# Pinning a root chain, summing modulation columns in pairs, and moving the odd blocks' sums in a two-layer trunk on one core

## The chip, the cores and the metric

The kernel runs on one core of a Trainium2 chip. A core has TensorE (matrix products), VectorE, ScalarE and GpSimd (element-wise work), SyncE, which issues the DMA transfers here, an on-chip memory (SBUF) and a small accumulation memory for TensorE's results (PSUM). The engines run side by side and wait for each other through semaphores. Each takes its own instructions strictly in the order in which they were written, so an instruction that waits holds everything behind it on its engine.

The metric is the device time of one execution in microseconds (us). Lower is better.

## The reference

The input x has 1024 tokens of 1024 numbers, the conditioning c has 1024. Two layers follow. Each has a mixer (layer A: an mLSTM, layer B: latent attention) and a feed-forward part (MLP) with a squared ReLU, each between two root-mean-square norms and each shifted, scaled and gated by vectors that are computed from c. Cut to what the change touches:

```python
c_act = jax.nn.silu(c)
for layer in range(DEPTH):
    sh1, sc1, g1, sh2, sc2, g2 = jnp.split(c_act @ mod_w[layer] + mod_b[layer], 6, axis=-1)
    h = modulate(rms_norm(x, norm_g[layer, 0]), sh1, sc1)
    y = mlstm_mixer(h, ...) if layer < N_A else mla_mixer(h, ...)
    x = x + g1[:, None, :] * rms_norm(y, norm_g[layer, 1])
    h = modulate(rms_norm(x, norm_g[layer, 2]), sh2, sc2)
    y = sq_relu_mlp(h, ffn_w1[layer], ffn_w2[layer])
    x = x + g2[:, None, :] * rms_norm(y, norm_g[layer, 3])
```

Here `modulate(h, shift, scale)` is `h * (1 + scale) + shift`, and `rms_norm` multiplies a token by one over the root of its mean square, then by a gain. All of it is computed in float32.

## The kernel before, in words

**Numbers and tiles.** Tokens are handled in 8 blocks of 128, features in 8 columns of 128 (`KD`). A float32 product is made of three products of a shorter type: each operand is split into a high half (a rounded copy, made by ScalarE) and a low half (the rest, made by VectorE), and `mm3` (L152) adds high times high, high times low and low times high. In the trace these are the lines L155, L156 and L157. Operands in SBUF live in 52 equal units (`U`). PSUM holds two wide tiles (`MM`, 1024 numbers, two banks) and four narrow ones (`SM`, 512 numbers, one bank).

**Order.** The program is traced from top to bottom, and a planner then writes the order of each engine: it runs a simulated clock with estimated costs and gives an engine that is free, by that clock, the earliest traced instruction that is ready. The order is fixed when the kernel is built. Two instructions of one engine can therefore stand in another order than in the source, and what the planner's clock held for ready can be late on the chip. `issue_after(ins)` is a request to the planner: instructions traced inside it are kept behind `ins` if they are of the same engine as `ins`.

**The front (`layer_a`, from L897).** The first four blocks of x are loaded (L407), then the weights that give shift and scale of the first norm, as four slabs of 2 MB: a slab has two neighbouring columns of shift and of scale, in eight transfers (`slab`, L961). ScalarE squares and sums each block (L926); VectorE turns the four sums of squares into inverse roots by a chain of small steps (`rsqrt`, L159 to L173); ScalarE scales the blocks with them (L930). Columns 0 and 1 of shift and scale are computed on TensorE, by 64 small matrix instructions with one column of c each (L995). Columns 2 to 7 are computed by `mod_sum` on VectorE: eight steps for a column, one for each 128 rows of the weights, each on 256 numbers (shift and scale), in two alternating accumulators (L982, L984), added by GpSimd (L985); TensorE then sums over the partitions (L992). `mod_col` (L988) adds the bias and the gain (L997, L999). `turned(k)` (L1001) does `mod_col`, transposes column k of the four blocks on TensorE (L183), applies scale and shift on ScalarE (L937) and splits the result into halves (L105, L106). The loop over k then feeds the value projection of the four blocks, 12 products a column, in four `SM` tiles that stay occupied until the last column (L1044). At k = 4 to 7 the other four blocks of x are loaded. At k = 7 a set of small constants (`late_consts`: positions, gate biases, norms) is loaded. After the loop come the evacuations of the values (`values`, `put_v`, L920) and the norm of the other four blocks.

**The mixers' last products.** After the mixer's core, each block n of a given order (0, 2, 4, 6, 1, 3, 5, 7) gets an output product (`out_proj`, 48 matrix instructions into an `MM` tile). In layer A its operand is first gated, transposed and split (`gate_split`, L1330, with L1338); three such blocks are traced ahead of the first product. `mixer_out` (L1145) follows each product: residual and norm (L178, L401, L402), store, and from time to time the norm of two finished blocks for the MLP (`h_norm`, L489: squares L494, root chain, scaling L497), after blocks n = 1, 3 and 5.

**The MLP.** It is a fast matrix scheme with seven products for a two-by-two cut of the operands. The token blocks are cut into even ones (0, 2, 4, 6) and odd ones (1, 3, 5, 7). `h_turn` (L444) transposes two blocks and applies shift and scale (L457). Even blocks are used as they are (left operands A11, A12), odd blocks also in sums with the even ones: `odd_sums` (L469, with L476 to L479) makes S1, S2, S3 and S4 on VectorE by four steps; `odd_high` and `odd_low` split them (L438, L442). Blocks 1 and 3 are the first odd pair (`odd_...(0)`), blocks 5 and 7 the second (`odd_...(2)`). While the odd blocks are made ready, TensorE runs the products that need even blocks alone: two products for each p from 0 to 7 (`up`, `up_product`, 24 matrix instructions for a p), whose results are taken out by L697 (ScalarE) and L690 (VectorE). Products 2 and 5 use two narrow tiles, the others one wide tile. In `mlp_begin` (L633) the odd blocks' steps are traced between these products. `w_first` (L504, L507, L509) and `w_step` (L540 to L589) load and split the weights, with some sums on GpSimd (L562, L563, L575, L582). Layer A and layer B share all of this code; in layer B the outputs' operands are split without a gate.

Of the kernel before, what the change touches and what calls it, by code (L numbers as in the profile page):

```python
# [21 lines left out]
P = 128  # L22
# [43 lines left out]
class Trunk:  # L66
# [31 lines left out]

    def SM(self):
        return self.pp.tile([P, 512], F32, tag="sm", name=self.nm("sm"), bufs=4)  # L100


    def split(self, hi, lo, src):
# [529 lines left out]
    def mlp_begin(self, l, odd):  # L633

        self.us = [self.dp.tile([P, 8 * 512], F32, name=f"us{l}_{p}", tag=f"us{l}_{p}") for p in range(self.NP)]
        self.ups = {}
        def up(p, *firsts):
            self.up_product(p, 1)
            self.up_product(p, 2)
            for f in firsts:  # L640
                next(self.first[f], None)

        self.odd_sums(0)
        up(0, 3, 4, 5)
        self.h_norm(5, 7)
        self.odd_high(0, "S2", "S3")
        up(1, 4, 5, 6)
        self.odd_high(0, "S1", "A22", "S4")
        self.odd_low(0, "S2", "S3")
        up(2, 5, 6, 7)  # L650
        self.odd_turn(2, [odd.pop(5), odd.pop(7)])
        self.odd_low(0, "S1", "A22", "S4")
        up(3, 6, 7)
        self.odd_sums(2)
        up(4, 7)
        self.odd_high(2, "S2", "S3", "S1")
        self.w_step()
        up(5)
        self.odd_high(2, "A22", "S4")
        self.odd_low(2, "S2", "S3")  # L660
        self.w_step()
        up(6)
        self.w_step()
        self.odd_low(2, "S1")
        self.w_step()
        up(7)
        self.w_step()
        self.odd_low(2, "A22", "S4")
        self.w_step()

    def up_product(self, p, s):
# [2 lines left out]
        S, V, G = self.S, self.V, self.G  # L674
        lo, hi = slice(0, 512), slice(512, 1024)
        if p not in self.ups:
            self.ups[p] = {"ps": None if p in (2, 5) else self.MM(), "x": [self.U("x")[:, :1024], None]}
        st = self.ups[p]
        ps = st["ps"][:, (lo, hi)[s - 1]] if s in (1, 2) and st["ps"] is not None else self.SM()
        w = self.w_take((0, p), s)  # L680
# [216 lines left out]
    def layer_a(self):  # L897
# [25 lines left out]
        def normed(xs, on_act=False):  # L923
            ssq = self.W("ssqs", [P, 4])
            for i, x in enumerate(xs):
                S.activation(self.U("h")[:, :D], x, AF.Square, accum_out=ssq[:, i : i + 1])  # L926
            r = self.rsqrt(ssq[:, : len(xs)], len(xs), 1.0 / D)
            for i, x in enumerate(xs):
                if on_act:
                    S.activation(x, x, AF.Copy, scale=r[:, i : i + 1])  # L930
                else:
                    V.tensor_scalar(out=x, in0=x, scalar1=r[:, i : i + 1], scalar2=None, op0=ALU.mult)

        def modulate(k, src, t, hi, lo, on_act):

# [35 lines left out]

            return slabs[k // 2][i // 2][:, i % 2, :, (k % 2) * P : (k % 2 + 1) * P]

        def mod_sum(k):

            u = self.U("acc")
            accs = [u[:, o : o + 2 * P].rearrange("p (s c) -> p s c", s=2) for o in (0, 2 * P)]
            for i in range(KD):
                src, acc = slab_part(k, i), accs[i % 2]
                c = self.cact[:, i : i + 1]  # L980
                if i < 2:
                    V.tensor_scalar(out=acc, in0=src, scalar1=c, scalar2=None, op0=ALU.mult)  # L982
                else:
                    V.scalar_tensor_tensor(out=acc, in0=src, scalar=c, in1=acc, op0=ALU.mult, op1=ALU.add)  # L984
            G.tensor_tensor(out=accs[0], in0=accs[0], in1=accs[1], op=ALU.add)  # L985
            sums[k] = accs[0]

        def mod_col(k, acc, ps):  # L988

# [28 lines left out]
            slab(2 * g)  # L1018
            self._raw()
        slab(6)  # L1020
        normed(xs[:4], True)
        for k in range(2, 4):
            mod_sum(k)
        w, acc = [], [None] * 4
        turned(0)
        for k in range(KD):
            if 1 <= k < 4:
                self._raw()
# [1 line left out]
                load_xs(k, k + 1)  # L1030
            if k == KD - 1:
                late = self.late_consts()
                next(late)
            if k % 3 == 0:
                w.append(self.take(("v", 0, k // 3)))
            if k + 4 < KD:
                mod_sum(k + 4)
            if k + 1 < KD:
                turned(k + 1)
            for tb in range(4):  # L1040
                if k == 0:
                    acc[tb] = self.SM()
                o = (k % 3) * VP
                self.mm3(acc[tb][:, :VP], self.hT_tb(hT, tb, k), tuple(u[:, o : o + VP] for u in w[k // 3]), k == 0, k == KD - 1)  # L1044
# [78 lines left out]
        finish(mods)  # L1123
        del hT
        order = self.ORDER
        pre = deque(self.gate_split(t, hn[t], sg) for t in order[:2])
        self.mixer_start(0, x_in, "x1")
        self.ahead, self.early = 0, 0
        w_out = [self.take(("wout", k)) for k in range(KD)]
        for n in range(NT):  # L1130
            if n + 2 < NT:
                pre.append(self.gate_split(order[n + 2], hn[order[n + 2]], sg))
            self.mixer_out(n, self.out_proj(pre.popleft(), w_out))


    ORDER = (0, 2, 4, 6, 1, 3, 5, 7)
# [8 lines left out]
    def mixer_out(self, n, y):  # L1145
# [4 lines left out]
        if n in (3, 5):  # L1150
            j = n - 3
            self.h_even(j, [hs.pop(t) for t in (2 * j, 2 * j + 2)])
        elif n == NT - 1:
            self.odd_turn(0, [hs.pop(1), hs.pop(3)])
        if n + 1 < NT:
            nxt = self.ORDER[n + 1]
# [2 lines left out]
        self.dma(out=x_out[tb * P : (tb + 1) * P, :], in_=xn)  # L1159
        if n in (1, 3, 5):  # L1160
            self.h_norm(*self.ORDER[n - 1 : n + 1])
        for p in range(self.BEGUN):
            if 0 <= n - 3 - p < 3:
                next(self.first[p], None)
# [684 lines left out]
```

## Time and profile before

| | us |
|---|---|
| median of 3 runs | 2317.43 (2316.24 to 2317.79) |
| the profiled execution, its own time | 2319.99 |
| its span in the trace | 2318.2 |
| TensorE busy | 2217.4 (96%) |
| VectorE busy | 1745.9 (75%) |
| ScalarE busy | 1012.0 (44%) |
| GpSimd busy | 472.0 (20%) |

PE stands for TensorE, PEld for its loading of weights, DVE for VectorE, ACT for ScalarE, POOL for GpSimd, SP for SyncE. L155 is line 155 of the kernel; where a helper records the instruction, the line is the helper's, and the names of the tiles tell the place. A row of waits reads "who waited <- for whom: total us, times, longest". A row of the timeline begins with its start and its length in us; in brackets stands the idle time of the engine before it and what ended that. A row of a table of stretches has, after the length, busy time and number of instructions for PE, PEld, DVE, ACT and POOL, then the granted TensorE clock as a share of full speed, the busy share of the DMA engines, and GB/s. A row of a group ends with its total busy time, the mean of one in ns, and the idle time before it. Ends of matrix instructions overlap, so the distance of two starts is the pace. A run's time is 1.8 us longer than the span of its trace here.

### The profile page before, as it was taken

The page shows a single profiled execution, that of the slowest core. Times are in us where ns is not written, and L with a number is a line of the kernel's source. Part 1 is how long each engine was busy: PE and PEld are TensorE (multiplying, and loading weights), DVE is VectorE, ACT ScalarE, POOL GpSimd, SP SyncE. Part 2 cuts the span into 40 slices and gives each one's busy share as a digit, 9 for nine tenths or more (in the row PEclk, how much of TensorE's full clock was granted, in tenths as well). Part 3 has the DMA queues.
Part 4 walks back from the last instruction along what each step waited for, and adds up shares of the span by engine and source line. Part 5 has one row for each costly group of instructions (what it writes and reads, how often), then busy time and mean ns, then how long its engine had stood idle before and what let it go on. Part 6 is the DMA issues. An engine that isn't in the chain of part 4 may idle for free. (4 is left out here: it accounts for less than half of the span.)

```text
span 2318.2 us, 29189 instructions
## 1 busy us (share of the span) xinstructions
PE 2217.4 (96%) x10786; PEld 1851.1 (80%) x10786; DVE 1745.9 (75%) x2792; ACT 1012.0 (44%) x1641; POOL 472.0 (20%) x322
## 2 busy tenths in 40 slices
PE   6999999998999999999999999999999999999998
PEld 5888887887777877777798989988777888777776
DVE  4585687667987767888999676665679877588888
ACT  3431366464444454333244545554634444633321
POOL 1000020003443333331021000000035433333300
PEclk9999999999999999999999999999999999999999
DMA  8376543143774465445322000022347545544452
GB/s 274 118 265 209 167 130 119 46 142 99 247 255 143 150 196 163 130 141 156 113 89 59 12 13 15 29 81 93 117 132 236 191 143 192 168 132 146 139 174 100
DMA packets 300070, 320.19 MB, mean 138 GB/s; under 512 B 16040, under 2 KB 252184, under 8 KB 299928
## 3 DMA queue, kind: packets, MB, share of 16 engines
q1 hardware_dynamic: 299928, 318.33, 43.4%
q8 instruction: 85, 1.39, 0.2%
q14 instruction: 57, 0.47, 0.1%
HBM read 245.85 MB, written 72.43 MB: 137 GB/s over the span
## 5 line engine op out<-in xcount | busy, mean ns | idle before, releaser
L155 PE MATMUL mm<-whi,uh 128*128 128x512 f32 x688 | 272.8, 397 | 12.6 <-DVE y L770 10.8
L157 PE MATMUL mm<-whi,ul 128*128 128x512 f32 x688 | 271.0, 394 | 1.2 <-DVE ul L764 1.2
L156 PE MATMUL mm<-wlo,uh 128*128 128x512 f32 x688 | 271.4, 394 | 0.0
L582 POOL TENSOR_TENSOR tt<-raw,tt 128x512 f32<-128x512 f32 x60 | 112.4, 1873 | 632.6 <-DVE wlo L555 632.6
L770 DVE TENSOR_TENSOR y<-y,mm 128x1024 f32<-128x1024 f32 (+1 forms) x161 | 193.2, 1206 | 49.7 <-PE mm L157 49.4
L155 PE MATMUL sm<-hSh,whi 128*128 128x512 f32 x544 | 216.2, 397 | 8.2 <-DVE x L690 7.9
L156 PE MATMUL sm<-hSl,whi 128*128 128x512 f32 x544 | 214.9, 395 | 0.0
L157 PE MATMUL sm<-hSh,wlo 128*128 128x512 f32 x544 | 213.8, 395 | 0.3 <-DVE wlo L555 0.3
L764 DVE TENSOR_TENSOR ul<-u,uh 128x896 fp32r<-128x896 f32 (+1 forms) x120 | 151.0, 1289 | 32.0 <-ACT uh L758 24.4
L555 DVE TENSOR_TENSOR wlo<-raw,whi 128x1024 fp32r<-128x1024 f32 x104 | 157.0, 1510 | 17.9 <-ACT whi L551 17.8
L690 DVE TENSOR_TENSOR x<-x,sm 128x512 f32<-128x512 f32 x196 | 130.9, 681 | 51.0 <-PE sm L157 48.1
L155 PEld LDWEIGHTS mm<-whi,uh 128*128 128x128 f32 x688 | 129.2, 188 | 49.2 <-DVE y L770 17.3
L562 POOL TENSOR_TENSOR tt<-raw,raw 128x512 f32<-128x512 f32 x32 | 57.3, 1791 | 496.9 <-PE sm L157 290.4
L157 PEld LDWEIGHTS mm<-whi,ul 128*128 128x128 f32 x688 | 129.2, 188 | 32.2 <-DVE ul L764 2.1
L156 PEld LDWEIGHTS mm<-wlo,uh 128*128 128x128 f32 x688 | 129.2, 188 | 29.3
L758 ACT CAST uh<-u 128x896 fp32r<-128x896 f32 (+1 forms) x120 | 108.0, 946 | 84.9 <-PE mm L157 66.8
L693 ACT ACTIVATE x<-x 128x1024 f32<-128x1024 f32 x64 | 67.8, 1059 | 149.6 <-DVE x L690 149.4
L155 PEld LDWEIGHTS sm<-hSh,whi 128*128 128x128 f32 x544 | 102.5, 188 | 35.4 <-DVE x L690 6.6
L265 DVE SCALAR_TENSOR_TENSOR acc<-modw,cact,acc 128x1024 f32<-128x1024 f32 x84 | 117.3, 1397 | 9.4 <-DMA modw<-in_kv_mod_w_dram 5.8
L551 ACT CAST whi<-tt 128x1024 fp32r<-128x1024 f32 x60 | 62.9, 1048 | 139.1 <-issue 62.2
L157 PEld LDWEIGHTS sm<-hSh,wlo 128*128 128x128 f32 x544 | 102.6, 189 | 25.2 <-DVE wlo L555 1.0
L587 ACT CAST w<-tt 128x512 fp32r<-128x512 f32 x60 | 37.2, 619 | 193.4 <-POOL tt L582 189.9
(407 smaller groups left out, 5975.2 us busy)
## 6 DMA issues: line engine op xcount, KB each, us to landing
raw<-in_ffn_w_dram SPq DMA_DIRECT2D x144, 512.0 KB, 4.9
u<-us SPq DMA_DIRECT2D x112, 448.0 KB, 4.2
us<-x SPq DMA_DIRECT2D x92, 512.0 KB, 2.6
modw<-in_mod_w_dram SPq DMA_DIRECT2D x80, 512.0 KB, 5.4
x<-xn SPq DMA_DIRECT2D x24, 512.0 KB, 3.3
x<-x SPq DMA_DIRECT2D x24, 512.0 KB, 4.0
x<-in_x_dram SPq DMA_DIRECT2D x16, 512.0 KB, 6.6
slab<-in_mod_w_dram SPq DMA_DIRECT2D x32, 256.0 KB, 5.9
```

Source lines behind the costliest of these rows:

```text
L155: mm(out, a[0], b[0], start=start, stop=False)
L156: mm(out, a[0], b[1], start=False, stop=False)
L157: mm(out, a[1], b[0], start=False, stop=stop)
L265: self.V.scalar_tensor_tensor(out=acc, in0=t, scalar=self.cact[:, k : k + 1], in1=acc, op0=ALU.mult, op1=ALU.add)
L551: S.copy(x[0], u)
L555: V.tensor_tensor(out=x[1], in0=u, in1=x[0].bitcast(F32), op=ALU.subtract)
L582: G.tensor_tensor(out=t1, in0=b21, in1=t2, op=ALU.subtract)
L690: V.tensor_tensor(out=dst, in0=src, in1=ps, op=ALU.add)
L693: S.activation(u, u, AF.Relu)
L758: S.copy(x[0], u)
L764: V.tensor_tensor(out=x[1], in0=u, in1=x[0].bitcast(F32), op=ALU.subtract)
L770: V.tensor_tensor(out=dst, in0=dst, in1=ps, op=ALU.add)
```

## The change

Five edits, in three places.

- **Front, order.** `normed` returns the last instruction of its root chain, and the first modulation sums and turns are traced inside `issue_after` of it: what they put on VectorE stays behind the chain. The late constants' loads are kept behind the load of block 7.
- **Front, sums.** `mod_sum(k, n)` sums n neighbouring columns at once, with one accumulator and no addition on GpSimd. Column 1 is summed alone, and 2 and 3, 4 and 5, 6 and 7 as pairs, with steps of 512 numbers. Column 0 alone stays on TensorE. Columns are turned in pairs.
- **Mixer A's last products.** Only the first block is gated ahead of the first product; the second and third are gated behind it.
- **Both mixers' last two products.** The first odd pair is turned after the seventh product (n = 6) and not after the eighth, and its sums and the halves of S2 and S3 are traced there, between the last two products. Blocks 5 and 7 are normed singly, each after its own residual. In `mlp_begin` the remaining steps of the odd blocks move up accordingly.
- **Products.** Product 6 also uses two narrow tiles.

```diff
-        self.odd_sums(0)
         up(0, 3, 4, 5)
-        self.h_norm(5, 7)
-        self.odd_high(0, "S2", "S3")
+        self.odd_high(0, "S1", "A22", "S4")
         up(1, 4, 5, 6)
-        self.odd_high(0, "S1", "A22", "S4")
-        self.odd_low(0, "S2", "S3")
-        up(2, 5, 6, 7)
         self.odd_turn(2, [odd.pop(5), odd.pop(7)])
         self.odd_low(0, "S1", "A22", "S4")
+        up(2, 5, 6, 7)
+        self.odd_sums(2)
         up(3, 6, 7)
-        self.odd_sums(2)
+        self.odd_high(2, "S2", "S3", "S1")
         up(4, 7)
-        self.odd_high(2, "S2", "S3", "S1")
+        self.odd_low(2, "S2", "S3")
+        self.odd_high(2, "A22", "S4")
...
-            self.ups[p] = {"ps": None if p in (2, 5) else self.MM(), "x": [self.U("x")[:, :1024], None]}
+            self.ups[p] = {"ps": None if p in (2, 5, 6) else self.MM(), "x": [self.U("x")[:, :1024], None]}
...
             r = self.rsqrt(ssq[:, : len(xs)], len(xs), 1.0 / D)
+            ins = self.last()
...
+            return ins
...
-        def mod_sum(k):
+        def mod_sum(k, n):
-            u = self.U("acc")
-            accs = [u[:, o : o + 2 * P].rearrange("p (s c) -> p s c", s=2) for o in (0, 2 * P)]
+            acc = self.U("acc")[:, : 2 * n * P].rearrange("p (s c) -> p s c", s=2)
+            o = (k % 2) * P
             for i in range(KD):
-                src, acc = slab_part(k, i), accs[i % 2]
+                src = slabs[k // 2][i // 2][:, i % 2, :, o : o + n * P]
...
-            G.tensor_tensor(out=accs[0], in0=accs[0], in1=accs[1], op=ALU.add)
-            sums[k] = accs[0]
+            for j in range(n):
+                sums[k + j] = acc[:, :, j * P : (j + 1) * P]
...
-        normed(xs[:4], True)
-        for k in range(2, 4):
-            mod_sum(k)
+        with self.tc.issue_after(normed(xs[:4], True)):
+            mod_sum(1, 1)
+            turned(0)
+            turned(1)
+            mod_sum(2, 2)
         w, acc = [], [None] * 4
-        turned(0)
...
                 late = self.late_consts()
-                next(late)
+                with self.tc.issue_after(self.last()):
+                    next(late)
...
-            if k + 4 < KD:
-                mod_sum(k + 4)
-            if k + 1 < KD:
+            if k % 2 and k + 1 < KD:
                 turned(k + 1)
+                turned(k + 2)
+                if k + 3 < KD:
+                    mod_sum(k + 3, 2)
...
-        pre = deque(self.gate_split(t, hn[t], sg) for t in order[:2])
+        pre = deque([self.gate_split(order[0], hn[order[0]], sg)])
...
-            if n + 2 < NT:
+            if 0 < n < NT - 2:
                 pre.append(self.gate_split(order[n + 2], hn[order[n + 2]], sg))
-            self.mixer_out(n, self.out_proj(pre.popleft(), w_out))
+            y = self.out_proj(pre.popleft(), w_out)
+            if n == 0:
+                pre.extend(self.gate_split(t, hn[t], sg) for t in order[1:3])
+            self.mixer_out(n, y)
...
-        elif n == NT - 1:
+        elif n == 6:
             self.odd_turn(0, [hs.pop(1), hs.pop(3)])
...
         if n in (1, 3, 5):
             self.h_norm(*self.ORDER[n - 1 : n + 1])
+        elif n >= 6:
+            self.h_norm(tb)
+        if n == 6:
+            self.odd_sums(0)
+            self.odd_high(0, "S2", "S3")
+            self.odd_low(0, "S2", "S3")
```

More of the change, by code (lines that the diff above doesn't have):

```diff
@@ L100, in SM, with last @@
         return self.pp.tile([P, 512], F32, tag="sm", name=self.nm("sm"), bufs=4)
+    def last(self):
+        return self.nc.cur_bb.bb.instructions[-1]
     def split(self, hi, lo, src):
@@ L641, in up @@
                 next(self.first[f], None)
-        self.odd_sums(0)
         up(0, 3, 4, 5)
-        self.h_norm(5, 7)
-        self.odd_high(0, "S2", "S3")
+        self.odd_high(0, "S1", "A22", "S4")
         up(1, 4, 5, 6)
-        self.odd_high(0, "S1", "A22", "S4")
-        self.odd_low(0, "S2", "S3")
-        up(2, 5, 6, 7)
         self.odd_turn(2, [odd.pop(5), odd.pop(7)])
         self.odd_low(0, "S1", "A22", "S4")
+        up(2, 5, 6, 7)
+        self.odd_sums(2)
         up(3, 6, 7)
-        self.odd_sums(2)
+        self.odd_high(2, "S2", "S3", "S1")
         up(4, 7)
-        self.odd_high(2, "S2", "S3", "S1")
+        self.odd_low(2, "S2", "S3")
+        self.odd_high(2, "A22", "S4")
         self.w_step()
         up(5)
-        self.odd_high(2, "A22", "S4")
-        self.odd_low(2, "S2", "S3")
+        self.odd_low(2, "S1")
         self.w_step()
@@ L663, in mlp_begin @@
         self.w_step()
-        self.odd_low(2, "S1")
+        self.odd_low(2, "A22", "S4")
         self.w_step()
@@ L667, in mlp_begin @@
         self.w_step()
-        self.odd_low(2, "A22", "S4")
         self.w_step()
@@ L972, in slab_part @@
             return slabs[k // 2][i // 2][:, i % 2, :, (k % 2) * P : (k % 2 + 1) * P]
-        def mod_sum(k):
-            u = self.U("acc")
-            accs = [u[:, o : o + 2 * P].rearrange("p (s c) -> p s c", s=2) for o in (0, 2 * P)]
+        def mod_sum(k, n):
+            acc = self.U("acc")[:, : 2 * n * P].rearrange("p (s c) -> p s c", s=2)
+            o = (k % 2) * P
             for i in range(KD):
-                src, acc = slab_part(k, i), accs[i % 2]
+                src = slabs[k // 2][i // 2][:, i % 2, :, o : o + n * P]
                 c = self.cact[:, i : i + 1]
-                if i < 2:
+                if i == 0:
                     V.tensor_scalar(out=acc, in0=src, scalar1=c, scalar2=None, op0=ALU.mult)
```

## The prediction

> **What bounds the kernel now.** I first read the page's busy times, then the waits of the two stretches that the diff touches, then a table of stretches, then each engine's timeline there.
>
> ```profile
> PE 2217.4 (96%) x10786; PEld 1851.1 (80%) x10786; DVE 1745.9 (75%) x2792; ACT 1012.0 (44%) x1641; POOL 472.0 (20%) x322
> ```
>
> TensorE is the bound nearly everywhere, so a change can only win where TensorE stands still or runs at a low clock. The waits name those places: the first 75 us, and the ends of both mixers (layer A near 540 us, layer B near 1690 us).
>
> ```profile
> ACT x L930 <- DVE rsy L172: 20.3, 1, 20.3
> DVE posf L1347 <- DMA posi<-in_positions_dram: 6.1, 1, 6.1
> ...
> PE mm L155 <- DVE x L690: 6.4, 3, 4.8
> ...
> PE mm L155 <- DVE x L690: 6.6, 3, 4.9
> ```
>
> ```profile
> core 0: us, PE busy (x) PEld busy (x) DVE busy (x) ACT busy (x) POOL busy (x), PEclk, DMA share, GB/s
> 52.00:62.00 10.00, 9.89 (x42) 9.40 (x41) 5.66 (x17) 3.70 (x6) 1.98 (x10) 0.52 0.00 0
> 69.20:73.60 4.40, 0.46 (x3) 0.22 (x2) 2.37 (x15) 4.40 (x13) 0.00 (x0) 0.79 0.84 239
> 73.60:80.00 6.40, 6.40 (x26) 6.40 (x27) 3.89 (x12) 0.79 (x5) 0.00 (x0) 0.61 0.23 60
> 497.00:507.00 10.00, 10.00 (x53) 8.32 (x52) 0.41 (x1) 4.14 (x9) 0.00 (x0) 1.00 0.57 158
> ```
>
> **The front.** This is the timeline of the first stage.
>
> ```profile
> 10.78 0.19 ACT L926 ACTIVATION_READ_ACCUMULATOR h<-x 128x1 f32 x1
> 10.93 13.79 PE L995 MATMUL mm<-cact,slab 128*128 128x1 f32 x64 [0.16 <-DMA slab<-in_mod_w_dram]
> 20.92 0.16 DVE L997 TENSOR_TENSOR modcol<-mm,bcols 128x2 f32<-128x2 f32 x1 [9.86 <-PE mm L995]
> 27.32 0.16 DVE L164 TENSOR_SCALAR rsv<-ssqs 128x4 f32<-128x4 f32 x1
> 30.96 0.16 DVE L172 SCALAR_TENSOR_TENSOR rsy<-rst,rsy 128x4 f32<-128x4 f32 x1
> 31.22 4.27 ACT L930 ACTIVATE x<-x,rsy 128x1024 f32<-128x1024 f32 x4 [20.25 <-DVE rsy L172]
> 38.33 1.12 PE L183 MATMUL mm<-ident,x 128*128 128x128 f32 x4 [0.37 <-DVE modcol L997]
> 38.34 0.77 ACT L937 ACTIVATE t<-mm,modcol 128x512 f32<-128x512 f32 x1
> 39.10 1.50 PE L155 MATMUL sm<-whi,hTh 128*128 128x344 f32 x4
> ...
> 57.87 0.49 PE L156 MATMUL sm<-wlo,hTh 128*128 128x344 f32 x1
> 58.15 0.49 PE L155 MATMUL sm<-whi,hTh 128*128 128x344 f32 x1
> ...
> 68.41 0.90 PE L157 MATMUL sm<-whi,hTl 128*128 128x344 f32 x4
> ```
>
> The sums of squares are complete at 10.97, but VectorE starts the root chain (L164 to L172) at 27.32: its order is fixed, and ahead of the chain stand the column result of L997, which waits for TensorE until 20.92, and modulation sums. Nothing of the blocks can be turned before the chain ends at 31.12.
>
> The pin puts the chain first. Its 11 steps lie 0.20 us apart (0.16 us of work and the way to the next), so from 11.1 they end at 13.3, and ScalarE's scaling (4.3 us) at 17.7. Column 0 is now alone on TensorE: 32 of the 64 products of L995 at 13.79/64 = 0.215 us are 6.9 us, to 17.8. Add 0.3 for L997 and L999, 1.1 for four transposes, 0.8 for L937 and 0.6 for the rounded half: the first value product starts near 20.6 instead of 39.1. **The start moves by 18.5 us.**
>
> What is then late next? Three candidates, from these rows.
>
> ```profile
> L984 DVE SCALAR_TENSOR_TENSOR acc<-slab,cact,acc 128x256 f32<-128x256 f32 x36 | 16.2, 502 | 0.0
> L265 DVE SCALAR_TENSOR_TENSOR acc<-modw,cact,acc 128x1024 f32<-128x1024 f32 x20 | 25.5, 1276 | 0.2
> L106 DVE TENSOR_TENSOR hTl<-t,hTh 128x512 fp32r<-128x512 f32 x8 | 5.5, 684 | 0.0
> ...
> L967 SPq DMA_DIRECT2D slab<-in_mod_w_dram x32: 367/368/969, 4.3 to 31.8; - x32
> ...
> DMA to landing us min/median/max: 4.5/5.9/6.1
> ```
>
> Transfers: the last slab is issued at 31.8 and lands near 37.7. VectorE: the trace has no step on 512 numbers of a slab; between 0.50 us for 256 and 1.28 for 1024 a straight line gives 0.76. Three pairs of eight steps are 18.3 us, column 1 (new on VectorE) 8 x 0.50 = 4.0; with hTl 5.5, the low halves of the weights 3.4 and 16 small column steps 2.4 that is 33.6 us, from 13.3 to 47. Behind it comes the last column's tail: transposes 1.1, L937 0.8, high half 0.6, low half 0.7, twelve products, 3.4 at the 0.28 us between the rows at 57.87 and 58.15, half of it at full clock: the stage ends at 52 to 54 if VectorE never rests. TensorE: the stage now takes 30.2 us from its first product (39.1) to its last (69.3); at that pace it would end at 50.8. I take 52, a **gain of 17 us**; 49 if the wide step costs only 0.60 as hTl's neighbours do, 61 under rival 2. That the wide steps also spare six additions on GpSimd is in this sum: columns no longer pass through a second engine.
>
> The late constants go behind the last block's load on SyncE. Today VectorE stands 6.1 us on posf (L1347) for one of them, with every later sum queued behind it. Their readers are the rotary tables, the gates and later layers, traced after this stage, so the later landing hides under the value products; I cost it at nothing beyond the front's sum. If posf still stood ahead of the pair sums, VectorE would hold until the blocks' loads have landed behind the slabs, and the front would lose about what rival 2 takes. From 73.6 on TensorE is busy 6.40 of 6.40 us, so what the front wins is kept. The 4.4 us before, where ScalarE (busy 4.40 of 4.40) does the squares of the other four blocks ahead of the evacuations that TensorE waits for, I leave as it is: 0, and 4.4 gained if the planner turns them round.
>
> **The mixer's start (layer A).** Only one block is gated ahead of the first product instead of three.
>
> ```profile
> 399.98 0.68 DVE L1338 TENSOR_TENSOR gt<-sm,sg 128x512 f32<-128x512 f32 x1
> 402.35 0.78 PE L155 MATMUL mm<-whi,aTh 128*128 128x512 f32 x1
> ```
>
> The first product needs gt, done at 400.66, and its two halves, 0.7 each: about 402.0 instead of 402.35, 0.4 us better. On the other side the second block's transposes (eight at the seam's 2.24/16, 1.1), gt, high and low half (0.7 each) can stand between the first two products, 3.2 lost; what then covers them is only what of the first product TensorE still has to do. I take 0, for both ends are small, and keep +0.4 and -3.2.
>
> **The seams.** Both layers show the same picture; this is layer A.
>
> ```profile
> 501.22 0.40 PE L155 MATMUL mm<-hSh,whi 128*128 128x512 f32 x1
> 507.24 0.15 DVE L164 TENSOR_SCALAR rsv<-ssq 128x1 f32<-128x1 f32 x1 [9.83 <-ACT xn L178]
> 509.09 1.23 DVE L476 TENSOR_TENSOR hs<-hr,hr 128x1024 f32<-128x1024 f32 x1 [0.17 <-ACT hr L457]
> 516.09 1.06 ACT L494 ACTIVATE h<-xn 128x1024 f32<-128x1024 f32 x1 [4.56 <-DVE xn L402]
> 525.83 2.19 ACT L497 ACTIVATE h<-xn,rsy 128x1024 f32<-128x1024 f32 x2 [0.53 <-DVE rsy L172]
> 527.36 2.24 PE L183 MATMUL sm<-ident,h 128*128 128x128 f32 x16
> 536.73 2.33 DVE L478 TENSOR_TENSOR hr<-hr,hr 128x1024 f32<-128x1024 f32 x1
> 545.23 0.67 DVE L690 TENSOR_TENSOR x<-x,mm 128x512 f32<-128x512 f32 x1
> 545.96 0.57 PE L155 MATMUL mm<-hSh,whi 128*128 128x512 f32 x1 [4.83 <-DVE x L690]
> 546.33 0.63 PE L156 MATMUL mm<-hSl,whi 128*128 128x512 f32 x1
> 549.71 0.39 PE L155 MATMUL mm<-hSh,whi 128*128 128x512 f32 x1
> ```
>
> VectorE rests 9.83 us up to 507.24 and is then full until 550; an evacuation (L690) that frees a bank for TensorE stands behind sums and low halves, and TensorE waits three times, 6.4 us. After the longest wait nine products lie 0.43 us apart instead of 0.23: another 1.8. So a seam costs 8.2 us in A and 8.4 in B.
>
> The change carries 7.5 us of VectorE's work (four sums of 1.23, four low halves at hTl's 0.68 less the overlap of neighbours) into the rest, behind the seventh product. Cover: the row 497 to 507, VectorE busy 0.41 us and ScalarE 4.14, under the eighth product. The turn that they need (16 transposes, 2.2 us of TensorE, and eight evacuations on ScalarE) moves with them. Without that cover, the sums would push the eighth residual back by their 7.5 us. The last two blocks' roots are taken singly, 2 x 8 steps for 11, but block 5's moves out of the crowd. Product 6 goes into single banks; that spares a wide bank, and I price it inside the seam. The low halves that move later (S1, A22, S4 of the first pair) and the second pair's stay in the crowd. If everything fits, both seams vanish: 16.6 us. The long wait with its slow clock, 6.6 us, is the part that hangs on the crowd; it falls where steps like L478 take 2.33 instead of 1.23, which stays. I take **6 us per seam, 12 together**, near that row, with 0 and 16.6 as ends and the loss of rival 3 beyond.
>
> **Sum.** The profiled execution took 2319.99 (span 2318.2): less 17 and 12 it is 2291.0. The median of the runs, 2317.43, lies 2.6 lower: 2288.
>
> **Rivals.**
> 1. *The seam's wait only moves.* Sums ahead of the eighth residual hold its wide bank, and the wait falls there. For it: VectorE's order is fixed; against: 9.83 us of rest take 7.5. Then 2288 + 12 = 2300. Chance 0.17.
> 2. *TensorE stays at half clock in the front,* since work comes thinner. At 0.28 us a product, 96 products are 27 us, 32 transposes at 1.12/4 are 9, seven columns of four small products at L995's pace 6: 42 from 18.5, the stage ends at 61, 8 gained instead of 17: 2297. For it: 52 to 62 ran at clock 0.52. A ScalarE order that sets the squares of blocks 4 to 7, loaded behind the slabs, ahead of columns costs about the same. Chance 0.15.
> The Trainium skill (TensorE: Matmul & The Clock Gate, Part 1: The HAM clock gate) says that an idle window of about 3.4 us halves the clock and that as much sustained work restores it. By that rule a front without rests recovers at once, as in the forecast, and one with rests between columns pays this rival's price. Our row disagrees with the quick recovery: busy 9.89 of 10 us, and still 0.52.
> 3. *Slower.* The second turn's transposes stand on TensorE after four products instead of six. They wait for blocks 5 and 7, scaled only at 528 now. If the sums on VectorE push the eighth residual back by 7.5, those blocks are ready at 535.5. TensorE begins the products at 501.2; four of them (twelve matmuls at 0.23) and the first turn bring it to the place at 514.5: 21 us of wait and 1.8 of slow clock in each seam, 45.6, less the 16.6 it replaces and 17 of the front: 2317.4 + 12 = 2329. It decides once a wait exceeds 15 us. Against it: block 5 leaves that root, and the planner places transposes when its own clock has the blocks ready. Chance 0.05.
> 4. *Nothing arrives:* the chain is early, but the planner orders the rest so that the stage still ends near 69, and the seams keep their waits: 2317. Against it: 18 us of VectorE's rest. Chance 0.04.
> 5. *More:* the 4.4 us at 69.2 and all of both seams go too: 2288 - 9 = 2279. Chance 0.09.
>
> **Numbers.** That leaves 0.50 for the forecast, whose own range is 2282 to 2295. A measurement here tells about 0.2%, 4.6 us, from no change. With rivals 1, 2 and 5 and the ends above, 2276 to 2308 leaves out rivals 3 and 4 and some tails, under 0.2. Faster: 0.50 + 0.17 + 0.15 + 0.09 = 0.91; within: 0.04; slower: 0.05.
>
> **What would show it.** L930 begins near 13.4 instead of 31.2, the first value product near 20.6, the stage ends between 49 and 54, and TensorE's wait for L690 falls under 3 us in each seam. I am wrong if the front ends past 60 (rival 2), if the same wait stands earlier in the seam (rival 1), or if transposes of the second turn wait long (rival 3).

## The result and the profile after

The changed kernel takes 2333.47 us (median of 4 runs, 2332.31 to 2334.58) against 2317.26 us (2316.24 to 2317.79) for the kernel before: ratio 1.0063, 95% interval 1.0050 to 1.0075. It is 16 us slower; 2288 was predicted. The profiled execution took 2332.31 us, its span 2330.5: 12.3 longer than the span before, whose trace is of a run 2.6 us above its median. Line numbers of the changed kernel are 4 higher than before up to about L640, the same from there to L926 (L690 stays L690), and 1 to 14 higher behind it; each experiment's differ by a few more, so go by the operation and its tiles.

The page's row of busy times says that no work came in:

```profile
PE 2215.5 (95%) x10758; PEld 1848.5 (79%) x10758; DVE 1746.1 (75%) x2786; ACT 1012.2 (43%) x1641; POOL 470.4 (20%) x316
```

TensorE is busy 1.9 us less in a span that is 12.3 us longer, so the loss is waiting. Three places on TensorE's timeline divide the 12.3 us. The first output product (L159, `mm<-whi,aTh`) begins at 394.81 instead of 402.35: the front gained 7.5. (One trace tells this to 2 us or so: with the same old front, it begins at 400.56 to 402.89 in e2_seam, e11_up6 and e14_seam_no6 below.) From there to the first down product (841.5 instead of 838.2) 10.8 are lost. The second mixer and its MLP lose another 9.0, for the last down product stands at 2319.8 instead of 2307.5, 12.3 late after 3.3.

**The front.** This is VectorE's timeline from the end of the root chain on (start, duration, engine, line, operation, tiles, count, and the idle time before it with what ended it).

```profile
12.30 0.16 DVE L176 SCALAR_TENSOR_TENSOR rsy<-rst,rsy 128x4 f32<-128x4 f32 x1
12.39 0.35 DVE L984 TENSOR_SCALAR acc<-slab,cact 128x256 f32<-128x256 f32 x1
18.85 0.16 DVE L999 TENSOR_TENSOR modcol<-mm,bcols 128x2 f32<-128x2 f32 x1 [6.11 <-PE mm L997]
...
19.44 3.09 DVE L986 SCALAR_TENSOR_TENSOR acc<-slab,cact,acc 128x256 f32<-128x256 f32 x6
...
36.67 0.69 DVE L110 TENSOR_TENSOR hTl<-t,hTh 128x512 fp32r<-128x512 f32 x1 [1.60 <-ACT hTh L109]
37.28 0.48 DVE L984 TENSOR_SCALAR acc<-slab,cact 128x512 f32<-128x512 f32 x1
...
40.88 3.89 DVE L986 SCALAR_TENSOR_TENSOR acc<-slab,cact,acc 128x512 f32<-128x512 f32 x5
...
49.21 0.69 DVE L110 TENSOR_TENSOR hTl<-t,hTh 128x512 fp32r<-128x512 f32 x1 [2.06 <-ACT hTh L109]
49.81 0.48 DVE L984 TENSOR_SCALAR acc<-slab,cact 128x512 f32<-128x512 f32 x1
```

The chain ends at 12.46, as early as predicted. But behind the first of eight steps of column 1's sum stands column 0's result (L999), which waits 6.11 us for TensorE; the other seven steps queue behind it. Later every pair's sum (the 0.48 us step opens one) stands behind the low half (L110) of the pair before, at 26.01, 37.28 and 49.81: it begins only when the pair before has come back from TensorE and ScalarE, and a pair takes 11.3 to 12.5 us. TensorE shows the other side of the same order:

```profile
19.16 0.88 PE L187 MATMUL mm<-ident,x 128*128 128x128 f32 x3 [0.35 <-DVE modcol L999]
22.58 1.01 PE L994 MATMUL mm<-ones,acc 128*128 128x1 f32 x4 [2.55 <-DVE acc L986]
23.46 1.51 PE L187 MATMUL mm<-ident,x 128*128 128x128 f32 x5
27.05 1.51 PE L159 MATMUL sm<-whi,hTh 128*128 128x344 f32 x4 [2.08 <-ACT whi L109]
33.65 1.02 PE L994 MATMUL mm<-ones,acc 128*128 128x1 f32 x8 [0.64 <-DVE acc L986]
44.92 1.84 PE L994 MATMUL mm<-ones,acc 128*128 128x1 f32 x8 [3.00 <-DVE acc L986]
56.43 1.02 PE L994 MATMUL mm<-ones,acc 128*128 128x1 f32 x8 [0.62 <-DVE acc L986]
65.86 0.80 PE L161 MATMUL sm<-whi,hTl 128*128 128x344 f32 x4
```

The first value product starts at 27.05 (before 39.10, predicted 20.6), and the stage's last ends at 66.66 (before 69.31, predicted 52): 12 us won at its start, 2.7 left at its end.

More of the front's 7.5 us comes from behind the stage. These are TensorE's next instructions there, before and in the changed kernel:

```profile
73.16 0.31 PE L183 MATMUL sm<-ident,rows 32*128 32x32 f32 x1 [3.85 <-DVE rsy L165]
67.41 0.25 PE L187 MATMUL sm<-ident,rows 32*128 32x32 f32 x1 [0.74 <-ACT vext L920]
```

Before, ScalarE squares the other four blocks from 68.47 to 72.74 and evacuates the values (L920) only from 72.64 on, and the first 17 products behind the gap are 0.29 us apart. In the changed kernel three of the four squares are done by 66.98, about the stage's end, the evacuations begin at 66.88, and the products are 0.16 apart. The transposes of the other blocks (`sm<-ident,x`) begin at 79.25 instead of 87.31: of these 8.1 us, 2.7 are the stage's end, 3.1 the shorter gap, and the rest the pace behind it. (The idle time of 3.85 us is 3.86 in e2, e11, e12 and e14, which have the old front too.)

**The seams.** In the table of waits (engine, tile and line, what it waited for; total, times, longest) the old wait for L690 is gone from both seams. These came instead, in A (470 to 560 us) and in B (1620 to 1710):

```profile
PE sm L187 <- ACT h L501: 8.5, 2, 7.2
PE mm L159 <- DVE xn L405: 4.9, 1, 4.9
...
PE sm L187 <- ACT h L501: 8.3, 2, 6.5
PE mm L159 <- DVE xn L405: 5.1, 1, 5.1
```

ScalarE's timeline in A shows why, and VectorE's and TensorE's what follows:

```profile
494.56 2.84 ACT L461 ACTIVATE hr<-sm,modcol 128x256 f32<-128x256 f32 x6 [6.09 <-PE sm L187]
497.27 1.05 ACT L182 ACTIVATE xn<-mm 128x1024 f32<-128x1024 f32 x1
...
512.41 1.15 ACT L501 ACTIVATE h<-xn,rsy 128x1024 f32<-128x1024 f32 x1 [2.69 <-DVE rsy L176]
```

```profile
498.44 0.15 DVE L168 TENSOR_SCALAR rsv<-ssq 128x1 f32<-128x1 f32 x1 [12.20 <-ACT xn L182]
...
500.24 1.28 DVE L405 SCALAR_TENSOR_TENSOR xn<-mm,rsy,row 128x1024 f32<-128x1024 f32 x1
```

```profile
493.36 0.60 PE L187 MATMUL sm<-ident,h 128*128 128x128 f32 x4
494.03 1.47 PE L187 MATMUL sm<-ident,h 128*128 128x128 f32 x12
501.58 0.80 PE L159 MATMUL mm<-hSh,whi 128*128 128x512 f32 x1 [4.90 <-DVE xn L405]
513.62 1.11 PE L187 MATMUL sm<-ident,h 128*128 128x128 f32 x4 [7.22 <-ACT h L501]
523.74 1.53 PE L187 MATMUL sm<-ident,h 128*128 128x128 f32 x12 [1.28 <-ACT h L501]
```

The seventh product was done near 484, but the square of its block (L182) stands on ScalarE behind six evacuations of the moved turn (L461), and these wait until 494.56 for transposes that TensorE has only at 493.36. So block 5's residual, VectorE behind it (12.20 us of rest), the wide bank that it frees (4.90) and the scaled block that the second turn's transposes want (7.22) are all late together. Block 5's root adds to the last of these: its steps stand among the sums and low halves on VectorE and take from 504.06 to 512.3, where they take 1.7 us in e3_turnlate below (490.16 to 491.85). The eighth block is late too: its product ended near 496.7, and its square ran at 508.62, behind casts that wait for the sums. The Trainium skill (TensorE: Matmul & The Clock Gate, under "Engine queue depths") says that ScalarE and VectorE take their instructions strictly first in, first out; these rows agree: an instruction that was ready at 484 ran at 497.

### The profile page after: what moved, and what is told of

The parts are those of the page before. It is cut to its first block, busy times and chain, and to the rows that moved or that the text cites. A ratio compares the mean times of both kernels' runs of the same rounds, so it can differ in the third digit from the quotient of the medians.

```text
span 2330.5 us, 29122 instructions
## 1 busy us (share of the span) xinstructions
PE 2215.5 (95%) x10758; PEld 1848.5 (79%) x10758; DVE 1746.1 (75%) x2786; ACT 1012.2 (43%) x1641; POOL 470.4 (20%) x316
## 5 line engine op out<-in xcount | busy, mean ns | idle before, releaser
L159 PE MATMUL mm<-whi,uh 128*128 128x512 f32 x688 | 273.2, 398 | 12.3 <-DVE y L770 10.4
L159 PE MATMUL sm<-hSh,whi 128*128 128x512 f32 x560 | 222.9, 398 | 8.9 <-DVE x L690 8.9
L160 PE MATMUL sm<-hSl,whi 128*128 128x512 f32 x560 | 221.6, 396 | 0.0
L161 PE MATMUL sm<-hSh,wlo 128*128 128x512 f32 x560 | 220.8, 396 | 0.0
L690 DVE TENSOR_TENSOR x<-x,sm 128x512 f32<-128x512 f32 x198 | 132.4, 682 | 60.3 <-PE sm L161 57.4
L159 PEld LDWEIGHTS mm<-whi,uh 128*128 128x128 f32 x688 | 129.4, 188 | 48.7 <-DVE y L770 14.2
L159 PEld LDWEIGHTS sm<-hSh,whi 128*128 128x128 f32 x560 | 105.9, 189 | 36.3 <-DVE x L690 6.9
L160 PEld LDWEIGHTS sm<-hSl,whi 128*128 128x128 f32 x560 | 105.9, 189 | 24.2
```

Of the source, the lines that this page charges most:

```text
L159: mm(out, a[0], b[0], start=start, stop=False)
L160: mm(out, a[0], b[1], start=False, stop=False)
L161: mm(out, a[1], b[0], start=False, stop=stop)
L690: V.tensor_tensor(out=dst, in0=src, in1=ps, op=ALU.add)
```

## The experiments

The kernel before ran beside each group on the same chip, with medians between 2317.3 and 2319.2; "+" is slower than it, "-" faster.

**1. The parts alone.** e1_front has the front's edits, e2_seam those between the last two products, e12_gate the gate's split.

> The kernel before with the front's edits alone: chain pinned, sums by pairs, columns 0 and 1 on TensorE, the last load held. Theory A (each part acts by itself through the order of its queues): the first output product began 7.5 us earlier in the changed kernel than before (394.8 against 402.3), so this one is 7.5 faster, about 2310; first value product near 27, pair sums still one behind each turn's halves. Rival (the front's new order also costs later, in the mixer or the MLPs): 2317 or more, though its first output product is early.

> The kernel before with the edits between the mixer's last two products alone: the first odd pair's turn, sums and two of its halves ahead of the eighth residual, the roots of the last two blocks single, product 6 in single banks, the second pair's work earlier in the first up products. Theory A: it carries the whole loss. From the first output product to the down products the changed kernel took 10.8 us longer in layer A and 8.1 in the later one, less 0.8 for the split of the gate's blocks: 17 to 18 slower, about 2335, with TensorE waiting for ScalarE's scaled blocks (L498) near 8 us and for VectorE's eighth residual (L402 here) near 5 us in each layer. Rival (the loss is one of the combination, as the front's edits leave banks or buffers later): under 8 slower, below 2325.

> The kernel before with the edit of the gate's split alone: the second and third blocks' splits behind the first output product. The prediction priced it at 0, between +0.4 and -3.2; the wait for the gate (4.8) was unchanged in the changed kernel, and the three parts together left 0.4 to it: within 1 of the kernel before. Rival (its transposes behind the first product cost): 2 to 3 slower.

e1_front: 2311.78, -6.3 (ratio 0.9974, 0.9965 to 0.9983). e2_seam: 2339.96, +21.9 (1.0096, 1.0081 to 1.0111). e12_gate: 2319.65, +2.4 (1.0012, 1.0002 to 1.0021). Together +18, near the change's +16, so it needs no cause in the combination. Most of the 7.5 us expected of the front arrived, and it was too little beside the 17 of the prediction. (The expectation of e1_front names columns 0 and 1 on TensorE; by its edit it is column 0 alone, as in the change.) e2_seam is slower than theory A said (17 to 18), with the same two waits. The gate's split missed its expectation of within 1: from the first output product to the last it takes 99.8 us (399.35 to 499.11). The kernels with the old split and the old seam (before, e1, e4, e5, e11, e13) take 97.7 to 98.7 there, so 1.1 to 2.1 of the 2.4 lie in this stretch; the rest I cannot place.

**2. The front's order.** e4_pin keeps the pinned chain and the held last load, but sums column by column as before, with columns 0 and 1 on TensorE (against the change):

```
         with self.tc.issue_after(normed(xs[:4], True)):
-            mod_sum(1, 1)
             turned(0)
-            turned(1)
-            mod_sum(2, 2)
+            for k in range(2, 4):
+                mod_sum(k)
```

> The kernel before with the root chain pinned ahead of the sums of columns 2 and 3 and the last load held, but with the sums column by column, two running sums and an addition on GpSimd as before, columns 0 and 1 on TensorE. Theory A (the pairs' sums, each behind the turn of the pair before on VectorE, give the gain back): shorter steps interleave, columns come about every 4 to 6 us, the stage ends at 52 to 60 and the kernel is faster than the one with the front's edits alone: 2300 to 2308. Rival (it is the pinned order of chain and sums itself, whatever the size of a sum): no better than the front's edits alone, 2310 or slower.

2315.76, -2.3 (0.9988, 0.9979 to 0.9998): no better than the pairs, and the theory of short steps missed. Its VectorE had a different obstacle. Column 0's turn is traced inside the issue_after of the chain, but column 1's is now outside it, and a result that waits for the last of the 64 small products stands ahead of the chain itself; as column 0's is kept behind the chain, it can only be column 1's.

```profile
24.34 0.16 DVE L1002 TENSOR_TENSOR modcol<-mm,bcols 128x2 f32<-128x2 f32 x1 [13.69 <-PE mm L1000]
24.53 0.16 DVE L1004 SCALAR_TENSOR_TENSOR modcol<-modcol,gcols 128x1 f32<-128x1 f32 x1
24.61 0.16 DVE L167 TENSOR_SCALAR rsv<-ssqs 128x4 f32<-128x4 f32 x1
```

So e4_pin does not test the size of a step. But in both kernels a column's result that waits for TensorE stands ahead of work that is ready: of the chain here, of column 1's sum there. e5_ahead keeps e1_front's work and holds the order by hand (against the change):

```
-            mod_sum(1, 1)
-            turned(0)
-            turned(1)
-            mod_sum(2, 2)
+            _, end = mod_sum(1, 1)
+            with self.tc.issue_after(end):
+                half, _ = mod_sum(2, 2)
+                turned(0, half)
+                turned(1, half)
...
-                turned(k + 1)
-                turned(k + 2)
-                if k + 3 < KD:
-                    mod_sum(k + 3, 2)
+                half, _ = mod_sum(k + 3, 2) if k + 3 < KD else (None, None)
+                turned(k + 1, half)
+                turned(k + 2, half)
```

Here mod_sum returns its fourth and its last step, and turned traces modulate (scale and shift, rounding, low half) inside an issue_after of the fourth step. That step is VectorE's, so of these it holds the low half alone.

> The kernel before with the front's edits (as in e1_front), and VectorE's order in it held by hand: column 0's finish stands behind all eight steps of column 1's sum, and the low halves of a pair of columns stand behind the first four steps of the next pair's sum instead of ahead of the sum. Same work. Theory A (the order on VectorE, each pair's sum behind the turn of the pair before, gives the front's gain back): columns 0 and 1 turn 3 us earlier, and pairs follow at 6 to 9 us instead of 11.4, until the last load lands near 47; last product of the stage near 56 to 59 instead of 66.7, so 7 to 10 faster than e1_front: 2302 to 2305. Rival (the stage is set by TensorE at its granted clock of 0.7 to 0.8 or by ScalarE's copies): within 3 of e1_front, 2309 to 2314.

2301.26, -17.4 (0.9929, 0.9914 to 0.9944), 11 faster than e1_front. Its VectorE and TensorE:

```profile
13.12 3.61 DVE L994 SCALAR_TENSOR_TENSOR acc<-slab,cact,acc 128x256 f32<-128x256 f32 x7
...
27.24 3.77 DVE L994 SCALAR_TENSOR_TENSOR acc<-slab,cact,acc 128x512 f32<-128x512 f32 x5
30.94 0.16 DVE L1008 TENSOR_TENSOR modcol<-mm,bcols 128x2 f32<-128x2 f32 x1
31.04 0.75 DVE L994 SCALAR_TENSOR_TENSOR acc<-slab,cact,acc 128x512 f32<-128x512 f32 x1
```

```profile
24.17 1.51 PE L160 MATMUL sm<-whi,hTh 128*128 128x344 f32 x4 [2.28 <-ACT whi L110]
...
53.55 0.80 PE L162 MATMUL sm<-whi,hTl 128*128 128x344 f32 x4
...
384.66 0.78 PE L160 MATMUL mm<-whi,aTh 128*128 128x512 f32 x1
```

The sum's steps now fill the time in which column results are on their way, the stage ends at 54.35, and the first output product is 17.7 earlier than before. From the chain to the last low half VectorE is busy 30.0 of 37.4 us (12.7 to 50.1); in the changed kernel it is 30.9 of 49.8 (12.4 to 62.2). Not all of the 17.7 is the stage: its end gives 15.0, the gap and the slow products behind it give another 5.7 (the other blocks' transposes begin at 66.60 instead of 87.31), and 3.0 are lost again on the way to the mixer's products. The instructions are the same and only VectorE's order was held (the other engines' orders follow it), so it was the order that took the front's gain.

**3. The seam's queues, one after another.** All three start from the changed kernel. e3_turnlate moves the turn behind block 5's residual and root; e6_castlate also moves the casts and low halves of S2 and S3 behind the eighth residual; e7_midturn also holds the turn's transposes in the middle of the eighth product.

```
 e3_turnlate, in mixer_out
-        elif n == 6:
-            self.odd_turn(0, [hs.pop(1), hs.pop(3)])
...
         if n == 6:
+            self.odd_turn(0, [hs.pop(1), hs.pop(3)])
             self.odd_sums(0)
 e6_castlate, besides
+        elif n == 7:
             self.odd_high(0, "S2", "S3")
             self.odd_low(0, "S2", "S3")
 e7_midturn, turn and sums not at n == 6 but in out_proj of the eighth product
         for k in range(KD):
+            if k == 4 and self.mid is not None:
+                self.odd_turn(0, [self.mid.pop(1), self.mid.pop(3)])
+                self.odd_sums(0)
+                self.mid, behind = None, self.tc.issue_after(self.turn_end)
...
+            with behind if k >= 4 else nullcontext():
...
```

> The changed kernel with one move: the first odd pair's turn (its 16 transposes and eight evacuations) is written behind block 5's residual and root instead of ahead of them, so that block 5's squares and scaling no longer stand behind the evacuations on ScalarE. Theory A (the ScalarE queue makes the loss): the wait for the wide bank (4.9) and the second turn's wait for block 5 (7.2) shrink to 0 to 2, and perhaps 4 of wait for block 7 appear: 6 to 10 faster per layer, 2313 to 2321. Rival 3 of the prediction (the four sums on VectorE push the eighth residual and block 7): little changes, over 2328, and the second turn's transposes still wait over 6 us. Rival (the banks of product 6 make the loss): within 3 of 2333.

> e3_turnlate with one more move: the high and low halves of S2 and S3 (ScalarE's four casts, which wait for VectorE's sums, and four subtractions) are written behind the eighth residual instead of ahead of it, so that its square (L182) no longer stands behind the casts. Theory (two queues hold block 7 back in e3_turnlate: ScalarE's casts by about 3.5 us, VectorE's four sums by 4.8): the wide bank's wait falls from 10.0 to 5 to 7 us in each layer, so 6 to 10 faster in all: 2312 to 2316. Rival (the sums on VectorE alone hold it): the wait stays over 9, 2320 or more.

> e6_castlate with the first odd turn's transposes held on TensorE in the middle of the eighth product (behind its first four of eight steps) and the sums written right behind them. Blocks 1 and 3 are scaled near 488.4 in e3_turnlate, but their transposes stand near 493, and VectorE rests 6.29 us for them. Theory (it is the turn's place at the end of the eighth product that makes the sums collide with the eighth residual): transposes near 490, sums from 493 to 498 in VectorE's rest, the eighth residual's square at once after its product, wide bank's wait under 2 us, seam as good as the forecast's 6 per layer against before: with the front's 6.3, 2298 to 2304. Rival (another wait takes its place: block 7's root, scaled only at 506 or later): 2308 to 2316.

e3: 2322.06, +4.0 (1.0018, 1.0009 to 1.0027), 11 less than the change. e6: 2318.69, 0.0 (0.9998, 0.9989 to 1.0008). e7: 2312.51, -6.2 (0.9975, 0.9965 to 0.9986). e3 came close to its range, but of its two waits only one shrank; e6 lies between its theory and its rival, with 7.6 us of wait where 5 to 7 were expected; e7 came out at its rival's time, though not through block 7's root. The waits of seam A, one fence per kernel in that order:

```profile
PE mm L159 <- DVE xn L405: 10.0, 1, 10.0
PE sm L187 <- ACT h L501: 0.8, 1, 0.8
```

```profile
PE mm L159 <- DVE xn L405: 7.6, 1, 7.6
PE mm L159 <- DVE x L690: 1.1, 1, 1.1
```

```profile
PE mm L160 <- DVE xn L416: 4.7, 1, 4.7
PE mm L160 <- DVE x L702: 1.1, 1, 1.1
```

Taking the evacuations out of block 5's way ends the 7.2 us wait of the transposes (8.5 to 0.8 in all): that cause is shown. The wait for the wide bank doubles at once, now for the eighth block, whose square stands behind casts that wait for the sums. With the casts out of its way the wait is 2.4 us less, with the turn earlier 2.9 less again. What is left in e7 is mostly no queue any more:

```profile
498.25 1.02 ACT L183 ACTIVATE xn<-mm 128x1024 f32<-128x1024 f32 x1 [1.74 <-PE mm L162]
```

```profile
500.18 0.15 DVE L169 TENSOR_SCALAR rsv<-ssq 128x1 f32<-128x1 f32 x1
...
501.96 1.28 DVE L416 SCALAR_TENSOR_TENSOR xn<-mm,rsy,row 128x1024 f32<-128x1024 f32 x1
```

The eighth product ends, its square begins at once, its root waits 0.8 us for the last of the sums, and the bank is free at 503.2. All but that 0.8 of the 5.0 us is the length of the chain itself. e7 with e5's front is e8_best; e9_narrow0 and e10_narrow036 put up product 0 into single banks too (`p in (0, 2, 5, 6)` and `p in (0, 3, 6)` instead of `(2, 5, 6)`), so that something can run meanwhile.

> e7_midturn with the front of e5_ahead. If both theories hold, the gains add: e5's gain over e1 below e7's time, 2288 to 2297, the time that was forecast for the change. If only one holds, 2300 to 2310.

> e8_best with up product 0 in single banks too (0, 2, 5 and 6). In e7_midturn TensorE's wait behind the eighth product (4.65) is the length of that block's own chain: square 1.0, root 1.75, evacuation 1.28, and the next up product wants its wide bank. In the kernel before the same chain lay under 16 transposes (2.2) and the 24 matmuls of product 2 in single banks (5.8); the changed order puts the transposes and half of product 0 ahead of the eighth product's end. Theory (the moved turn took the cover of the eighth block's chain away): with 24 matmuls in single banks behind the eighth product the wait of 4.6 falls under 1 in each layer: 6 to 10 faster than e8_best, 2290 to 2294. Rival (VectorE's backlog behind the sums and the scaling of block 7 sets the pace): the wait reappears at the next up products, within 3 of e8_best.

> As e9_narrow0, with products 0, 3 and 6 in single banks instead of 0, 2, 5 and 6: the single banks spread over the eight. Theory: the same cover behind the eighth product, 2290 to 2296. Rival: within 3 of e8_best.

e8: 2300.60, -18.1 (0.9923, 0.9909 to 0.9938), the time for only one theory holding: the front's holds, and e7's mended seam adds nothing measurable to e5's front with the old seam (2301.26), though e8 also has product 6 in single banks and e5 has not (e13 below has). e9: 2296.47, -20.8 (0.9908, 0.9893 to 0.9923), between theory and rival. e10: 2293.07, -24.2 (0.9892, 0.9877 to 0.9906), within it. The wait behind the eighth product is gone in both, and others have taken part of its place: in e9 for the two halves of a weight (3.1 us for `whi`, 1.7 for `wlo`), in e10 for a bank that transposes need (3.2 us, `sm L188 <- ACT x L709`).

**4. The bank.** e11_up6 is the kernel before with one number of the change, product 6 in single banks:

```
-            self.ups[p] = {"ps": None if p in (2, 5) else self.MM(), ...
+            self.ups[p] = {"ps": None if p in (2, 5, 6) else self.MM(), ...
```

e14_seam_no6 is e2_seam without it, and e13_held_up6 is e5's front with it, the seam's order as before.

> The kernel before with product 6 in single banks alone. In it TensorE waits 4.8 us in each layer for an evacuation (L690) that frees a wide bank late in the up products. If the bank is what is short there, single banks for product 6 take most of it away: 4 to 8 faster in both layers together, 2309 to 2313. If VectorE's crowd of sums and halves is what is late, the wait comes at another product: within 2 of 2317.

> e2_seam with product 6 in its wide bank as before: only the new order of turn, sums, halves and roots. If the parts add, the order alone costs e2's 22 and the 11 that product 6 gives: 2346 to 2352. If product 6's gain is one that the new order cannot use (the wait that it removes, L690, is gone there anyway, taken by the earlier waits): within 4 of e2_seam, 2334 to 2343.

> The front of e5_ahead (17.4 faster than before) and product 6 in single banks (11.1 faster in e11_up6), with the seam's order otherwise as before: the odd turn, its sums and halves behind the eighth residual. If the two act apart from each other the gains add, 28.5: 2287 to 2291, the forecast's time without the seam's new order. If the seam's gain needs something of the old front, or the clock takes part of it back: 2294 or more.

e11: 2306.22, -11.1 (0.9951, 0.9936 to 0.9966), two thirds of the 16.6 that the prediction counted in both seams and more than the 4 to 8 expected, with no turn and no sum moved. Where TensorE had run 36 matmuls in wide banks in a row behind the wait of 4.83, its order now has 9 or 10 matmuls in single banks between the next dozens in a wide one, and the evacuation has that time: the waits for such evacuations (L690, here L694) fall from 6.4 to 1.6 us in A and from 6.6 to 1.8 in B. e14: 2338.61, +19.4 (1.0082, 1.0065 to 1.0099): its interval overlaps that of e2, so in the new order product 6 gives nothing that can be measured, and the parts do not add there. e13: 2289.58, -29.7 (0.9872, 0.9857 to 0.9887): in the old order they do, 17.4 + 11.1. The waits for up products in wide banks over the whole run, before and in e13:

```profile
PE mm L155 <- DVE x L690: 13.0, 6, 4.9
```

```profile
PE mm L160 <- DVE x L695: 3.3, 4, 1.0
```

e13 is the fastest kernel here, 29.7 us below the kernel before and 44 below the changed one. e8 has the same front and the same product 6 and, besides, the gate's split (2.4 alone) and the seam's new order as e7 mends it. It is 11 us slower than e13: of the new seam, nothing that was tried here pays.

## Why the prediction was wrong

The forecast added 17 us of gain in the front and 12 in the seams. Alone, the front's edits gain 6.3 (e1_front), and the seams' edits lose 21.9 (e2_seam).

- **The chain and the start.** "From 11.1 they end at 13.3" is right (12.46). "The first value product starts near 20.6" failed by 6.5. Column 0's small products end 1.0 later than forecast (18.8). Another 3.8 is its fourth transpose: on TensorE it stands behind column 1's sum over the partitions (22.58), and that waits for the seven steps which VectorE has behind column 0's result. The last 1.7 is the high half of the weights, which ScalarE makes at 25.95 to 26.99; the sum had no term for it. I had placed column 1's sum in VectorE's work, not in its order.
- **The stage's end.** The sizes held: a wide step takes 0.75 us, 0.76 was estimated. The step that failed is "the stage ends at 52 to 54 if VectorE never rests". It took the sum of VectorE's work for its time. In the changed kernel VectorE rests while each pair goes over TensorE and ScalarE and back, because the next sum stands behind that pair's low half. The condition was named and never tested against the order. e5_ahead comes nearest to it (7.4 us of rest instead of 18.9), and there 54.35 and 17.4 us stand where 52 and 17 were forecast. That 17.4 is so near to 17 is partly luck: the stage's end gives 15.0 of it.
- **The 4.4 us behind the stage,** "I leave as it is: 0, and 4.4 gained if the planner turns them round". The planner did much of this: the shorter gap (3.1) and the faster products behind it gave more than the stage's end (2.7). So more than half of the front's 7.5 came from a term that the forecast had put at nothing.
- **Rival 2's half clock** is there, as a consequence. In the changed kernel the table of stretches (busy time of TensorE, weight loads, VectorE, ScalarE, GpSimd, then granted clock and DMA) shows it after the thinnest four microseconds:

```profile
41.00:45.00 4.00, 0.99 (x5) 0.73 (x5) 3.63 (x5) 0.00 (x0) 0.00 (x0) 0.95 1.03 405
45.00:49.00 4.00, 3.56 (x16) 3.16 (x16) 0.64 (x4) 1.22 (x2) 0.00 (x0) 0.50 0.46 115
49.00:53.00 4.00, 3.77 (x13) 3.77 (x14) 3.72 (x6) 1.48 (x3) 0.00 (x0) 0.50 0.00 0
53.00:57.00 4.00, 3.38 (x19) 3.13 (x17) 3.14 (x5) 0.00 (x0) 0.00 (x0) 0.77 0.00 0
```

  The rests come from VectorE's order, which the rival did not name. That the gain of 8 which it left is near the 6.3 of e1_front is luck: it has the stage end at 61, and the stage ended at 66.66, nearer to the 69 of rival 4. The Trainium skill (TensorE: Matmul & The Clock Gate, Part 1: The HAM clock gate) has the full clock back after about 3.4 us of sustained work; here TensorE was busy 3.56 and 3.77 of 4 us, and the clock stayed at 0.50 for both stretches.
- **Late constants** at nothing: right, posf is computed at 62.18 without a wait, and e5 keeps the load where the change put it. **The mixer's start** at nothing: e12_gate puts 2.4 there, inside the bound of 3.2 that was kept.
- **The seams: two steps failed.** The first is "The turn that they need (16 transposes, 2.2 us of TensorE, and eight evacuations on ScalarE) moves with them". I priced what moved, and not what is queued behind it: block 5's square, ready near 484, ran at 497.27. The cover that I quoted, VectorE's rest from 497 to 507, was real, but the sums could not use it, since their turn came only at 493; then they fell on the eighth residual instead (e3, e6).
- The second is that the long wait "is the part that hangs on the crowd", and that product 6 "spares a wide bank, and I price it inside the seam". The reverse holds: e11 takes the wait away with no sum and no half moved in the source, by the bank alone. That the 12 us forecast for the seams are nearly that edit's 11.1 is luck; the turn and the sums, which I took for the gain, are the loss.
- **Rival 3** had the right picture, the second turn's transposes parked on TensorE and slower as the outcome (2329; measured 2333), at a chance of 0.05 and with half of the cause: it had VectorE's sums push the eighth residual, which they did, but the longest wait (7.22) was for block 5, which the ScalarE queue held. Rival 1's wait for a wide bank came as well, 4.9 us a seam, first for block 5's residual and, with that way cleared, for the eighth (10.0 in e3). Rival 3's threshold of 15 us was set too high: 7.2 and 4.9 us a seam were enough, since the front gave 6 to 7 and not 17.

## What to carry to other kernels

An engine's idle time covers moved work only if the order of its queue lets that work stand there: read what stands ahead of each instruction and what that waits for, before adding up durations. When a step is moved, list for every engine it uses what is now behind it; evacuations that wait for a transpose hold everything on ScalarE, however short they are. And when a wait names an evacuation that frees a bank, try another bank before moving the work.

## What the runs showed of the hardware

Product 6 in single banks is worth 11.1 us in the old order (e11) and nothing that can be measured in the new one (e14 against e2): in this kernel the worth of a bank depends on which wait ends last. In the changed kernel the half clock outlasted two stretches of 4 us with TensorE busy for 89% and 94% of them, and in the kernel before it held at 0.50 from 57 to 61 us with TensorE busy all of the time.
